# One encoder layer on one core: the order of projection blocks, operand stacks and value transposes in the attention stage

## The chip, the core and the metric

The kernel runs on one core of a Trainium2 chip. The metric is the device time of one execution in microseconds. Three runs of the kernel before give a median of 1028.46 us (1026.88 to 1028.7). The engines are named as in the profile: PE is TensorE (matrix multiply), PEld its weight loads, DVE VectorE, ACT ScalarE, POOL GpSimd, SP the engine that issues most DMAs. L389 is line 389 of the kernel.

## What is computed

One layer of an encoder over 1024 tokens of width 1024, in float32: one projection feeds two kinds of attention, group A (8 heads in two sets of four, a window of 128 tokens to each side) and group B (8 heads, a neighbourhood in a 16 by 64 grid). An output projection and a gated feed-forward block with a convolution follow.

```python
hn = rmsnorm(h, norm_mix[l])
proj = jnp.einsum('bsd,de->bse', hn, w_in[l])
qa, ka, va, qb, kb, vb = jnp.split(proj, splits, axis=-1)
...
o_a = window_gqa_sink(qa, ka, va, sink[l])
o_b = neighbourhood_attention(qb, kb, vb, rpb[l])
mix = jnp.concatenate([rmsnorm(o_a, norm_a[l]), rmsnorm(o_b, norm_b[l])], axis=-1)
h = h + jnp.einsum('bse,ed->bsd', mix, w_out[l])
hn = rmsnorm(h, norm_ffn[l])
h = h + conv_gated_mlp(hn, w_gate[l], w_up[l], conv_w[l], conv_b[l], w_down[l])
return rmsnorm(h, norm_final)
```

## The kernel before

**Arithmetic.** Each float32 operand is split into a rounded high part and the rest. A product is then three matmuls (high by high, rest by high, high by rest: lines 178 to 180). Everything is kept transposed, features on the partitions and tokens along the free dimension.

**Two streams on TensorE.** TensorE's instructions keep the program's order (`manual_schedule`, line 136). The other engines' order is made when the kernel is built, by readiness and priority, so an instruction of theirs can run well ahead of its place in the text. During attention the program interleaves two streams:

- *Filler.* A generator, `rest()` (line 775), runs the jobs. Jobs 3 to 17 are projections (`Project`), each of one 128-column tile; the eight behind them, `OutA`, are the first half of the output projection. A job has 16 *blocks* of three 512-column matmuls (line 177), eight for each half of the tokens. A half is collected in one of two PSUM banks called "pj" and copied out by VectorE (`evacuate`, line 239). Job 17 does both halves side by side; on its way it also splits group A's result for `OutA` (`split_part`, line 608, with line 611 on VectorE).
- *Attention units.* There are 16 window units for group A (two sets of eight) and 32 grid units for group B (four for each of eight heads, units 16 to 47). A unit is a list of events: a score step (two matmuls, line 389, then the softmax: bias and minimum at line 412, exponent at 416, normalisation on GpSimd at 420), a transpose step (lines 452 or 526, then the split at 426 and 427) and a value step (lines 457 and 458, or 537 and 538). Scores run ahead of the transposes by a few steps. The value step that is issued is always that of the transpose before (`pend`).

**Rates.** `RATES` (line 34) sets how many blocks are filled in during each set of window units (first two entries) and each grid head (the other eight). Every event adds its share to `debt`, and whole blocks are issued from it (lines 929 to 932).

**Posts.** When a job's blocks are done, it waits in `waiting` until `settle(age)` (line 758) posts it; the age is the number of the block within the next job. A post needs places for operands (`big(..., "op")`, 14 buffers of 128 by 1024). `needs(m)` says how many; `live["op"]` counts those in use and is lowered by 4 at the end of a grid head (line 933). The rule for the age is in line 765: 3 (`LAG`), 13 for job 3, 1 (`SOON`) for job 17.

- Jobs 6, 9, 12 and 15 are the values of two grid heads each. Their post is `split_v` (line 322): four transposes into a "pj" bank, two copies (line 333) and two subtractions (line 334), and the same again for the second half of the tokens eight settles later (line 347).
- Jobs 7, 8, 10, 11, 13, 14, 16 and 17 are query and key of the grid heads 0 to 7. Their post is `split_qk` (line 296). ScalarE makes the high part in two halves (line 301), VectorE the rest (line 302). Four DMAs on SP's queue then stack high and rest, query and key, into q, ka and kb. Two of them overwrite what the first two read:

```python
nc.sync.dma_start(f32(q[0:64, :]), f32(a[0:64, :]))
nc.sync.dma_start(f32(q[64:128, :]), f32(b[0:64, :]))
mark["stacked"] = nc.sync.dma_start(f32(b[0:64, :]), f32(a[64:128, :]))
nc.sync.dma_start(f32(a[0:64, :]), f32(b[64:128, :]))
```

A head's first score needs all four. `run_q` (line 876) makes sure only that the post has been issued ahead of it in the program. The bias tiles of a grid head are built on GpSimd (lines 490 and 491), on the same queue as the normalisation of line 420.

Of the kernel before, what the change touches and what calls it, by code (L numbers as in the profile page):

```python
# [30 lines left out]

LAG, LATE, SOON = 3, 13, 1
FILL0, FILL1 = 22, 14
RATES = [41, 50, 21, 21, 22, 22, 13, 19, 19, 16]
SPARE = (3, 6)
AHEAD = 4
GRID_AHEAD = 6
# [20 lines left out]
def hybrid_layer(tc, xT, w_first, w_in, w_out, w_gate, w_up, w_down, small, sink, rpb, consts, rope, out):  # L58
    nc = tc.nc
    with ExitStack() as ctx:  # L60
# [11 lines left out]
        slots = {"xg": 16, "op": 14, "mix": 8, "rstd": 1}  # L72
# [28 lines left out]
        flat = lambda t, n: t[:, 0:n * 384].rearrange("p (k c) -> p k c", c=384)  # L101
# [51 lines left out]
        def behind(*names):  # L153

            stack = ExitStack()
            for n in names:
                stack.enter_context(tc.issue_after(mark[n].ins))
            return stack
# [590 lines left out]
        live = {"op": 0}  # L749
        needs = lambda m: 2 if m < 6 and m % 3 else 2 if m >= 6 and m % 3 == 0 else 3  # L750
        waiting = []
# [6 lines left out]
        def settle(age):  # L758

            for item in list(later):  # L760
                item[0] -= 1
                if item[0] <= 0:
                    later.remove(item)
                    item[1]()
            while waiting and (len(waiting) > 1 or age >= (LATE if waiting[0].m == 3 else SOON if waiting[0].m == 17 else LAG)):
                m = waiting[0].m
                if live["op"] + needs(m) > slots["op"]:
                    break
                live["op"] += needs(m)
                with behind(*["stack", "low"] * (m == 3)):  # L770
                    waiting.pop(0).post()
# [3 lines left out]
        def rest():  # L775
            for i, job in enumerate(jobs):
                if i + 1 < len(jobs):
                    with behind(*[["spread", "root"], ["stack"]][i] if i < 2 else []):
                        jobs[i + 1].load()
                for n, _ in enumerate(job.run()):  # L780
                    yield True
                    if i == 0:
                        if n == 8:
                            with behind("copied"):
                                for p in first[:2]:
                                    make_stacks(p)
                        continue
                    if n == REST and i + 1 < len(jobs):
                        jobs[i + 1].load_rest()
                    settle(n)  # L790
                    if (i, n) in aux:
                        aux[i, n]()
                if i == 0:
                    with behind("stack", "copied"):
                        jobs[1].load_rest()
                    with behind("weights", "weights low"):
                        make_stacks(third)
                if isinstance(job, Project):
                    waiting.append(job)
                while len(waiting) > 2:  # L800
                    settle(0)
                    if len(waiting) > 2:
                        yield False
# [34 lines left out]
        def fill(n):  # L838
            while n > 0 and next(filler, False):
                n -= 1  # L840
# [11 lines left out]
        fill(FILL0)  # L852
        rates = RATES
        flat = []
# [13 lines left out]
        def q_until(u, limit):  # L868
            nonlocal qpos
            res = []  # L870
            while qpos < len(queue_q) and queue_q[qpos][0] <= u and len(res) < limit:
                res.append(queue_q[qpos])
                qpos += 1
            return res

        def run_q(items):
            nonlocal debt
            for u, s in items:
                while any(m not in done for m in flat[u][2]):
                    assert next(filler)  # L880
                    debt -= 1
                s()

        sums = {}

        def square_b(u):

            if u == 40:
                sums["b"] = big("sqb", "op")
                for h in range(2):  # L890
                    nc.scalar.activation(sums["b"][:, tsl(h)], mix[4][:, tsl(h)], AF.Square)
            s2 = tmp("sq")
            for h in range(2):
                nc.scalar.activation(s2[:, tsl(h)], mix[5 if u == 40 else 6][:, tsl(h)], AF.Square)
                nc.vector.tensor_tensor(sums["b"][:, tsl(h)], sums["b"][:, tsl(h)], s2[:, tsl(h)], op=ALU.add)

        pend = None
        for i, item in enumerate(q_until(1, 4 + AHEAD)):
            run_q([item])
            fill(i % 2 + 1)  # L900
        fill(FILL1 - 12)
        for u in range(len(flat)):
            q, t, need, kind = flat[u]
            events = []
            if kind == 0:
                mine = q_until(u + 2, 4 if u < 14 else 99)
                for ts in t:
                    events += [("t", ts), ("v", None)]
                for i, item in enumerate(mine):
                    events.insert(min(EVA[i], len(events)), ("q", item))  # L910
                rate = [RATES[u // 8] / 8 / len(events)] * len(events)
            else:
                rate = []
                for ts in t:
                    mine = q_until(len(flat) - 1, 1 if events or u > 16 else GRID_AHEAD - 3)
                    events += [("t", ts)] + [("q", item) for item in mine] + [("v", None)]
                    rate += [RATES[2 + (u - 16) // 4] / 8 / (2 + len(mine))] * (2 + len(mine))
            if u in (40, 44):
                square_b(u)
            for (what, e), per in zip(events, rate, strict=True):  # L920
                if what == "t":
                    nxt = e()
                elif what == "v":
                    if pend is not None:
                        pend()
                    pend = nxt
                else:
                    run_q([e])
                debt += per
                due = max(0, int(debt))  # L930
                fill(due)
                debt -= due
            live["op"] -= 7 if u in (7, 15) else 4 if u >= 16 and u % 4 == 3 else 0
        with tc.high_priority(offset=500), behind("high"):
            nc.scalar.activation(warm, eps, AF.Sqrt)
        fill(2)
# [420 lines left out]
        for i, f in enumerate(FO[HEAD:]):  # L1357
            u = Gated(f)
# [269 lines left out]
```

## Time and profile before

| what | us |
|---|---|
| median of three runs | 1028.46 (1026.88 to 1028.7) |
| profiled execution, its time | 1031.37 |
| profiled execution, its span | 1029.6 |
| DVE busy | 834.8 |
| ACT busy | 563.8 |
| first score of grid head 0 | 170.58 |
| first score of grid head 6 | 300.15 |
| first score of grid head 7 | 325.10 |
| last score | 343.23 |

The span runs from the first to the last instruction. All times in the rows are counted from its start. A row of the timeline gives start, duration, engine, line, operation, output and inputs, and in brackets the idle time before it and what ended that. A row of the windows gives the stretch, its length, the busy time of PE, PEld, DVE, ACT and POOL with the number of instructions, the granted clock of TensorE, the DMA share and GB/s. Matmuls overlap, so what one costs is read from start to start. A wait for several semaphores is put down to the one that came last by the profile.

### The profile page before, as it was taken

How to read it: one execution, taken by the hardware profiler on the slowest of the kernel's cores; microseconds unless marked ns; L12 is line 12 of the kernel's file. 1: busy time of each engine (PE TensorE's matmuls, PEld its weight loads, DVE VectorE, ACT ScalarE, POOL GpSimd, SP SyncE). 2: the span in 40 equal slices, each digit the busy share in tenths (PEclk: the TensorE clock that was granted, in tenths of full speed). 3: DMA queues.
4: the chain of work that ended last, by engine and by line, in shares of the span. 5: the costliest groups of instructions: out<-in, count | busy, mean ns of one | idle time of the engine just before them, and what ended most of it. 6: DMA issues, size and time to landing. Idle time of an engine off the chain costs nothing.

```text
span 1029.6 us, 14879 instructions
## 1 busy us (share of the span) xinstructions
PE 1012.8 (98%) x5094; PEld 893.1 (87%) x5094; DVE 834.8 (81%) x1570; ACT 563.8 (55%) x1081; POOL 107.5 (10%) x188
## 2 busy tenths in 40 slices
PE   9999999999989999999999999999999999999997
PEld 8898888899878988888888888888888888888886
DVE  7889887768978699999987877786787777996675
ACT  8567776657666555555535444443444654554451
POOL 0233342322332100000000000000000000000002
PEclk9999999999989999999999999999999999999998
DMA  7224022333325258313443332333322788966644
GB/s 291 76 77 97 28 72 62 82 82 82 83 61 158 82 166 270 103 41 123 151 187 102 113 117 99 113 113 113 102 98 107 263 303 287 309 243 231 217 161 164
DMA packets 68220, 144.94 MB, mean 141 GB/s; under 512 B 8240, under 2 KB 18736, under 8 KB 68144
## 3 DMA queue, kind: packets, MB, share of 16 engines
q1 hardware_dynamic: 58064, 118.82, 36.1%
q10 hardware_dynamic: 10080, 25.17, 6.3%
q8 instruction: 40, 0.66, 0.3%
q14 instruction: 36, 0.29, 0.1%
HBM read 103.58 MB, written 28.57 MB: 128 GB/s over the span
## 4 chain that ended last, share of the span: by engine, by line
PE 82%; DVE 11%; ACT 3%; DMA 3%; issue 2%; DVEq 0%; POOL 0%; SPq 0%; ACTq 0%
PE pj L178 7%; PE dn L1011 6%; PE dn L1012 6%; PE dn L1013 6%; PE pj L180 6%; PE pj L179 6%; PE x L1011 6%; PE x L1012 6%; PE x L1013 6%; PE y L1011 3%; PE y L1013 3%; PE y L1012 3%; PE s L389 3%; PE z L1013 2%; PE z L1011 2%
## 5 line engine op out<-in xcount | busy, mean ns | idle before, releaser
L1011 PE MATMUL x<-hg,whi 128*128 128x512 f32 x352 | 133.7, 380 | 1.8 <-ACT gs L1053 1.8
L1012 PE MATMUL x<-hg,whi 128*128 128x512 f32 x352 | 133.4, 379 | 0.0
L1013 PE MATMUL x<-hg,wlo 128*128 128x512 f32 x352 | 133.4, 379 | 0.0
L1011 PE MATMUL dn<-xd,whi 128*128 128x512 f32 (+1 forms) x330 | 120.8, 366 | 0.0
L1012 PE MATMUL dn<-xd,whi 128*128 128x512 f32 (+1 forms) x330 | 120.5, 365 | 0.0
L1013 PE MATMUL dn<-xd,wlo 128*128 128x512 f32 (+1 forms) x330 | 120.5, 365 | 0.0
L416 ACT ACTIVATE p<-p,nm 128x385 f32<-128x385 f32 (+3 forms) x128 | 75.1, 587 | 58.0 <-DVE nm L412 55.5
L178 PE MATMUL pj<-xgh,whi 128*128 128x512 f32 x245 | 100.5, 410 | 1.0 <-DVE v L334 0.7
L985 ACT ACTIVATE whi<-ws 128x512 fp32r<-128x512 f32 (+1 forms) x100 | 60.7, 621 | 72.0 <-DVE ws L1125 16.6
L420 POOL TENSOR_SCALAR p<-p,sm 128x384 f32<-128x384 f32 (+1 forms) x128 | 78.3, 625 | 198.3 <-DVE sm L418 158.9
L179 PE MATMUL pj<-xgl,whi 128*128 128x512 f32 x245 | 93.6, 382 | 0.0
L180 PE MATMUL pj<-xgh,wlo 128*128 128x512 f32 x245 | 93.6, 382 | 0.0
L985 ACT ACTIVATE whi<-raw 128x512 fp32r<-128x512 f32 (+1 forms) x102 | 60.9, 610 | 47.3 <-PE x L1012 20.7
L427 DVE TENSOR_TENSOR pl<-pt,ph 128x384 fp32r<-128x384 f32 (+2 forms) x108 | 63.6, 589 | 25.6 <-ACT ph L426 24.0
L986 DVE TENSOR_TENSOR wlo<-ws,whi 128x512 fp32r<-128x512 f32 (+1 forms) x100 | 66.6, 680 | 19.7 <-ACT whi L985 19.5
L1011 PEld LDWEIGHTS x<-hg,whi 128*128 128x128 f32 x352 | 66.5, 189 | 11.9 <-ACT gs L1053 2.6
L1334 DVE TENSOR_TENSOR xd<-xd 128x512 fp32r<-128x512 f32 x77 | 52.3, 687 | 29.2 <-ACT xd L1333 28.8
L1333 ACT ACTIVATE xd<-xd 128x512 fp32r<-128x512 f32 x77 | 47.6, 627 | 51.8 <-DMA xd<-x 50.9
L1448 POOL TENSOR_TENSOR h<-h,wide 128x256 f32<-128x256 f32 (+1 forms) x6 | 5.4, 917 | 673.8 <-ACT wide L1444 673.8
L1013 PEld LDWEIGHTS x<-hg,wlo 128*128 128x128 f32 x352 | 66.5, 189 | 9.5
L1012 PEld LDWEIGHTS x<-hg,whi 128*128 128x128 f32 x352 | 66.5, 189 | 9.4
L986 DVE TENSOR_TENSOR wlo<-raw,whi 128x512 fp32r<-128x512 f32 (+1 forms) x102 | 66.2, 668 | 3.7 <-ACT whi L985 3.7
(267 smaller groups left out, 2532.9 us busy)
## 6 DMA issues: line engine op xcount, KB each, us to landing
xd<-x SPq DMA_DIRECT2D x77, 256.0 KB, 5.0
raw<-in_w_down_dram SPq DMA_DIRECT2D x72, 256.0 KB, 4.5
raw<-in_w_gate_dram SPq DMA_DIRECT2D x22, 512.0 KB, 3.4
raw<-in_w_up_dram SPq DMA_DIRECT2D x22, 512.0 KB, 3.5
x<-c ACTq DMA_DIRECT2D x22, 512.0 KB, 2.6
raw<-in_w_in_dram SPq DMA_DIRECT2D x30, 256.0 KB, 2.7
raw<-in_w_down_dram SPq DMA_DIRECT2D x36, 192.0 KB, 4.2
x<-t ACTq DMA_DIRECT2D x11, 512.0 KB, 2.6
```

The source lines that it names most:

```text
L178: nc.tensor.matmul(ps, w[0], mv(x[0][:, tsl(h)]), start=first, stop=False)
L179: nc.tensor.matmul(ps, w[0], mv(x[1][:, tsl(h)]), start=False, stop=False)
L180: nc.tensor.matmul(ps, w[1], mv(x[0][:, tsl(h)]), start=False, stop=last)
L416: nc.scalar.activation(p[:, j, 0:e], p[:, j, 0:e], AF.Exp, bias=nm, scale=-1.0, accum_out=sm[:, j:j + 1])
L420: nc.gpsimd.tensor_scalar(p[:, i, 0:m], p[:, i, 0:m], sm[:, i:i + 1], 1.0, op0=ALU.mult, op1=ALU.mult)
L427: mark["rest"] = nc.vector.tensor_tensor(pl[:, 0:n], ps[:, 0:n], f32(ph[:, 0:n]), op=ALU.subtract)
L985: nc.scalar.activation(hi, src, AF.Copy)
L986: nc.vector.tensor_tensor(lo, src, f32(hi[:, :, :]), op=ALU.subtract)
L1011: nc.tensor.matmul(ps, w[0], x[0], start=first and i == 0, stop=False, skip_group_check=True)
L1012: nc.tensor.matmul(ps, w[0], x[1], start=False, stop=False, skip_group_check=True)
L1013: nc.tensor.matmul(ps, w[1], x[0], start=False, stop=last and i == len(ws) - 1, skip_group_check=True)
L1334: nc.vector.tensor_tensor(lo, f32(lo), f32(hi), op=ALU.subtract)
```

## The change

Four edits, all in the order in which the attention stage is issued; the instructions stay the same.

```diff
-RATES = [41, 50, 21, 21, 22, 22, 13, 19, 19, 16]
+RATES = [41, 50, 22, 22, 23, 22, 13, 19, 17, 15]
...
-            while waiting and (len(waiting) > 1 or age >= (LATE if waiting[0].m == 3 else SOON if waiting[0].m == 17 else LAG)):
+            while waiting and (len(waiting) > 1 or age >= (LATE if waiting[0].m == 3 else SOON if waiting[0].m >= 16 else LAG)):
                 m = waiting[0].m
-                if live["op"] + needs(m) > slots["op"]:
+                if live["op"] + needs(m) > slots["op"] or m in (6, 9, 12, 15) and age % 8 not in (3, 4):
                     break
...
                 s()
+                if u >= 16 and u % 4 == 3 and s is flat[u][0][-1]:
+                    live["op"] -= 3
...
-            live["op"] -= 7 if u in (7, 15) else 4 if u >= 16 and u % 4 == 3 else 0
+            live["op"] -= 7 if u in (7, 15) else 1 if u >= 16 and u % 4 == 3 else 0
```

1. The rates of grid heads 0, 1 and 2 rise by one block each; those of heads 6 and 7 fall by two and one.
2. Job 16 (query and key of head 6) may be posted at age 1, as job 17 was before, instead of 3.
3. The values of the grid heads (jobs 6, 9, 12, 15) are posted only at ages 3, 4, 11 and 12: near the top of a half.
4. Of the four places that a grid head gives back, three (q, ka, kb) are counted free as soon as its last score has been issued, and one (its values) at the head's end as before.

## The prediction

> **What bounds the kernel now.** I read the page first, then the waits of TensorE, then its timeline around each of those waits, then the chain of waits behind them.
>
> ```profile
> PE 1012.8 (98%) x5094; PEld 893.1 (87%) x5094; DVE 834.8 (81%) x1570; ACT 563.8 (55%) x1081; POOL 107.5 (10%) x188
> ```
>
> ```profile
> PE s L389 <- DMA ka<-kb: 2.5, 1, 2.5
> ...
> PE s L389 <- DMA kb<-ka: 1.5, 2, 0.8
> PE s L389 <- DVE nm L412: 1.1, 2, 0.9
> ...
> PE pj L178 <- DVE v L334: 0.7, 1, 0.7
> ```
>
> TensorE is the bound: it is busy for 1012.8 of 1029.6 us. This change removes and adds no instruction, so all it can win is TensorE's idle time, and clock lost through it. Most of that sits in front of scores (line 389), where a head's stacked operands (q, ka, kb) come late by DMA. The timeline shows where:
>
> ```profile
> 296.47 0.49 PE L526 MATMUL pt<-cst,p 128*128 128x128 f32 x3
> 296.72 0.46 PE L178 MATMUL pj<-xgh,whi 128*128 128x512 f32 x1
> 297.02 0.38 PE L179 MATMUL pj<-xgl,whi 128*128 128x512 f32 x1
> 297.24 0.38 PE L180 MATMUL pj<-xgh,wlo 128*128 128x512 f32 x1
> 300.15 0.35 PE L389 MATMUL s<-ka,q 128*128 128x256 f32 x1 [2.54 <-DMA ka<-kb]
> 301.30 0.58 PE L389 MATMUL s<-kb,q 128*128 128x256 f32 x1 [0.80 <-DMA kb<-ka]
> ```
>
> This is head 6's first score. A 512-column matmul starts 0.22 us after the one before it (297.02 to 297.24) and a 256-column one is taken as half of that, so the second score matmul was due at 297.24 + 0.22 + 0.11 = 297.57. It started at 301.30: **3.73 us late**. Then the clock falls (the last columns are granted clock, DMA share and GB/s):
>
> ```profile
> 300.00:304.00 4.00, 3.05 (x8) 2.55 (x9) 2.93 (x5) 1.23 (x4) 2.83 (x4) 0.59 0.18 38
> 304.00:308.00 4.00, 4.00 (x14) 3.42 (x13) 1.84 (x5) 1.50 (x4) 0.00 (x0) 0.56 0.00 0
> ```
>
> At 0.59 and 0.56 the two stretches lose 0.41 x 4 + 0.44 x 4 = 3.4 us of clock. About 0.4 of it falls in time in which TensorE idled anyway, so **3.0 us** is lost on top of the wait.
>
> ```profile
> 323.85 0.38 PE L180 MATMUL pj<-mgh,wlo 128*128 128x512 f32 x1
> 325.10 0.35 PE L389 MATMUL s<-ka,q 128*128 128x256 f32 x1 [0.87 <-DVE nm L412]
> 326.12 0.38 PE L389 MATMUL s<-kb,q 128*128 128x256 f32 x1 [0.67 <-DMA kb<-ka]
> ```
>
> Head 7's first score: due 323.85 + 0.33 = 324.18, started 326.12, so **1.94 us**. No drop of the clock follows.
>
> ```profile
> 192.27 0.60 PE L329 MATMUL vt<-cst,t 128*128 128x128 f32 x4
> ...
> 195.48 0.45 PE L178 MATMUL pj<-xgh,whi 128*128 128x512 f32 x1 [0.66 <-DVE v L334]
> ```
>
> Job 9's second group of value transposes takes a "pj" bank two blocks before job 11's second half needs one; TensorE waits **0.66 us** for VectorE to empty it. The four places add up to 3.73 + 3.0 + 1.94 + 0.66 = **9.3 us**.
>
> **The change part by part.** TensorE's order is the program's. I worked out by the loop's own arithmetic (rates, debt, ages, count of places) which block of a job stands before which score, with both sets of numbers. For the kernel before, that list agrees with the order of TensorE's rows from job 3's start to the last score.
>
> *The rates* move three blocks of filler from the time of heads 6 and 7 into heads 0 to 2. In all, 281 blocks still stand ahead of the end of the units. Head 6's first score moves from 7 blocks behind job 16's end to 10, and 2 scores, 2 groups of transposes and 2 value pairs also come between. Head 7's moves from 10 blocks behind job 17's end to 12, with 1 score, 1 group and 2 pairs. Prices from job 16's last block:
>
> ```profile
> 288.72 0.33 PE L537 MATMUL o<-ph,v 128*128 128x384 f32 x1
> ...
> 289.04 0.38 PE L178 MATMUL pj<-xgh,whi 128*128 128x512 f32 x1
> ...
> 289.69 0.38 PE L526 MATMUL pt<-cst,p 128*128 128x128 f32 x2
> 289.83 0.41 PE L389 MATMUL s<-ka,q 128*128 128x384 f32 x1
> ...
> 290.24 0.38 PE L178 MATMUL pj<-xgh,whi 128*128 128x512 f32 x1
> ...
> 314.11 0.46 PE L178 MATMUL pj<-mgh,whi 128*128 128x512 f32 x1
> ```
>
> From start to start a value pair takes 0.32 us, a block 0.65, a score 0.41 or less, three transposes 0.25 (296.47 to 296.72). Head 6 so gains 3 x 0.65 + 2 x (0.32 + 0.25 + 0.41) = 3.9 us of lead, head 7 2 x 0.65 + 2 x 0.32 + 0.25 + 0.41 = 2.6. What the stacks need is read from the chain of waits:
>
> ```profile
> 294.57 0.94 DVE kb L302
> ...
> 295.52 2.87 DMA q<-kb
> ...
> 298.40 2.85 DMA kb<-ka
> ...
> 318.33 0.74 DVE kb L302
> ...
> 319.10 2.93 DMA q<-kb
> ...
> 322.04 4.03 DMA kb<-ka
> ```
>
> Two DMAs in series follow the second subtraction. Head 6: job 16's blocks end at 289.69, the stacks land at 298.40 + 2.85 = 301.25, so 11.6 us are needed. There were 297.46 - 289.69 = 7.8, and there will be 11.7: the wait is gone with 0.1 us to spare. Head 7: from 314.11 to 326.07, 12.0 us needed; there were 324.07 - 314.11 = 10.0, and there will be 12.6.
>
> *Posting job 16 at age 1* moves two activations, two subtractions and four DMAs on SP's queue up by two blocks: with the rates, five. But the activation already ran before the old place (block 3 of job 17, TensorE at 294.65):
>
> ```profile
> 292.06 0.72 ACT L301 ACTIVATE ka<-t,cst 128x512 fp32r<-128x512 f32 x1
> ```
>
> Only the end of job 16 holds it, so this edit wins between 0 and the 1 us that the two halves were apart; I take 0. On SP nothing else is issued between the stack's DMAs of head 6, so no transfer is overtaken there. Head 7's stacks keep their place, with a load of w_out's weights between their DMAs.
>
> *Places freed at the last score*: the count only. Without it job 15's post (block 212) would count 12 + 3 = 15 of 14 places and slip; with it, it stays. No other post changes by it: 0.
>
> *Value transposes at a half's top*: of jobs 6, 9, 12 and 15 only job 9 moves, its groups from blocks 126 and 134 to 132 and 140. Each then stands four or more blocks (2.6 us and the attention between) ahead of the next use of a "pj" bank: the 0.66 us go. Four copies and four subtractions move with them, beside job 10's split. That split feeds head 2's first score 23 blocks later, which covers it; were the cover gone, the cost is the 0.7 us back.
>
> **What is late next.** Without the stalls, the same work must fit in less time. VectorE (third busy column):
>
> ```profile
> 230.00:284.00 54.00, 53.86 (x319) 48.41 (x318) 45.25 (x110) 38.89 (x92) 17.39 (x25) 1.00 0.31 80
> 284.00:332.00 48.00, 42.91 (x231) 37.54 (x230) 38.57 (x91) 32.34 (x78) 14.54 (x20) 0.93 0.40 113
> ...
> 430.00:500.00 70.00, 69.11 (x321) 60.20 (x320) 69.64 (x108) 41.00 (x66) 0.00 (x0) 1.00 0.23 74
> ```
>
> Its 38.57 us in 284 to 332 would stand in 48 - 8.7 = 39.3 us: 98%. The trace shows no such load in this stage, so I bound it. If it runs as in 430 to 500 (99%, TensorE idle 0.89 of 70), it costs 0.5 us. If it could be no denser than in 230 to 284 (84%), the stretch would take 46 us and give back 6.6. Some of that work (the split of the first group's mix, line 611) isn't urgent and can slide into the slack behind 332, so I take 1.3, nearer the dense row. GpSimd is the other candidate:
>
> ```profile
> 298.31 1.96 POOL L490 TENSOR_TENSOR xb<-cst,rr 128x384 f32<-128x384 f32 x1 [3.35 <-DVE nm L412]
> ...
> 301.37 1.47 POOL L420 TENSOR_SCALAR p<-p,sm 128x384 f32<-128x384 f32 x2
> ```
>
> The normalisation of head 5's last pair queues behind a bias build. Its first half is through by about 302.4, for a transpose that without the stall is due some 6 us of such pieces behind 297.46, near 303.4: 1 us to spare. I take 0.5 for this and the thin margin of head 6 (from 0 to 2). Sum: 9.3 - 1.3 - 0.5 = 7.5 us. The profiled execution took 1031.37 us (span 1029.6), so it would be 1023.9; the median of the runs shown is 2.9 lower, and 7.5 off 1028.46 is **1021.0**.
>
> **The clock, by trace and rule.** The drop followed idle stretches of 2.54 and 0.80 us, and none followed 0.87 and 0.67. The Trainium skill ("TensorE: Matmul & The Clock Gate", the sections on the clock gate and its oscillation) says that the gate looks at free-running windows of some 3.4 us and that gaps shorter than that keep the clock. The trace disagrees with the second half: no single gap here was that long. By the first half, whether a stall of this size costs clock depends on where the window falls, and may differ from run to run.
>
> **The rivals.**
> *The timed runs have no drop of the clock.* Then 3.0 us can't be won: 7.5 - 3.0 = 4.5, 1024.0. For: the profiled execution is 2.9 us above the median, the size of the drop. Against: nothing else tells the runs apart. 20%.
>
> *VectorE is the bound where the stalls were.* It gives back 6.6 instead of 1.3: 1026.3. For: 98%. Against: the row of 430 to 500. 12%.
>
> *Nothing is won*: the waits move to another head or place in full, 1028.5 (1026.4 to 1030.5). For: ScalarE's and VectorE's orders are made anew at each build, and no row shows the new ones. Against: job ends and DMAs in series set these waits, and both keep their durations. 12%.
>
> *Slower: the splits of line 611 get ahead of head 6's second subtraction in VectorE's queue.*
>
> ```profile
> 296.75 0.67 DVE L611 TENSOR_TENSOR mgl<-mixa,mgh 128x512 fp32r<-128x512 f32 x1
> ```
>
> All eight of them, and job 17's two weight subtractions of like length, would delay it by 10 x 0.67 = 6.7 us. The wait becomes 11.6 + 6.7 - 11.7 = 6.6 against 3.73, the drop of the clock stays, and with 1.8 given back elsewhere and 2.6 won at head 7 and the values, it is 2.9 + 1.8 - 2.6 = 2.1 us slower: 1030.6. It turns slower from nine such instructions on. Against: line 611 writes places that job 17 frees two blocks at a time, and it ran behind the subtraction before. 9%.
>
> **How the numbers follow.** The forecast, 1021.0, has 47%; its own range, with 0.5 to 3.6 given back, is 1019.6 to 1022.8. With the case without the drop and most of the VectorE case, 1018.5 to 1027.0 holds 8 in 10. A measurement of this kernel tells some 0.2% (2.06 us) from no change: faster means below 1026.4. That holds the forecast, the first rival and most of the second: 0.78; same 0.12; slower 0.10.
>
> **What would show it.** TensorE's waits list the DMAs of ka and kb with under 0.5 us in all; the granted clock is 1.00 from 296 to 308; the row of "pj" waiting for the value subtraction is gone; the span from head 6's job to the end of the units is some 9 us shorter, and the rest of the trace is shifted by that. It is wrong if line 389 still waits over 2 us, if line 526 or 537 begins to wait, or if the gain vanishes later, between 430 and 500.

## The result and the profile after

The changed kernel takes 1021.99 us (median of six runs, 1021.22 to 1024.5) against 1029.33 for the kernel before (six runs): a ratio of 0.9926, with a 95% interval of 0.9912 to 0.9939. That is 7.3 us less; 7.5 were forecast.

The profiled execution spans 1022.7 us. It lost 1.75 us where nothing was changed, ahead of the first value step, and is the slowest of its six runs. Most of that is the clock's: by the trace's clock records it first rose to full 10.0 us behind the start, against 7.1 in the kernel before, and in the 2.9 us between TensorE ran nine matmuls instead of 15. So the attention stage is read by itself. These are its first and last value steps in TensorE's timeline, first of the kernel before:

```profile
70.00 0.38 PE L457 MATMUL o<-ph,v 128*128 128x512 f32 x1
...
357.45 0.28 PE L538 MATMUL o<-pl,v 128*128 128x256 f32 x1
```

and then of the changed kernel:

```profile
71.75 0.38 PE L457 MATMUL o<-ph,v 128*128 128x512 f32 x1
...
350.64 0.28 PE L538 MATMUL o<-pl,v 128*128 128x256 f32 x1
```

287.45 us have become 278.89: the stage is 8.56 us shorter. Where they came from is in TensorE's waits of the changed kernel (line numbers behind 882 are two higher):

```profile
PE x L1013 <- ACT gs L1055: 1.6, 2, 0.9
...
PE s L389 <- DMA kb<-ka: 1.0, 2, 0.6
...
PE s L389 <- DVE nm L412: 0.2, 1, 0.2
```

Of the four rows shown in the prediction, the wait for ka (2.5 us) and the one of "pj" for the value subtraction (0.7) are gone, the one for kb has gone from 1.5 to 1.0, and that for line 412 from 1.1 to 0.2. The timeline around head 6's and head 7's first scores:

```profile
297.18 0.38 PE L180 MATMUL pj<-xgh,wlo 128*128 128x512 f32 x1
...
299.47 0.27 PE L389 MATMUL s<-ka,q 128*128 128x256 f32 x1
300.35 0.38 PE L389 MATMUL s<-kb,q 128*128 128x256 f32 x1 [0.61 <-DMA kb<-ka]
...
319.35 0.36 PE L389 MATMUL s<-ka,q 128*128 128x256 f32 x1
320.06 0.38 PE L389 MATMUL s<-kb,q 128*128 128x256 f32 x1 [0.36 <-DMA kb<-ka]
```

Head 6's second score matmul starts 0.88 us behind the first, where 0.11 would do: 0.8 us late instead of 3.7. Head 7's starts 0.71 us behind its first, where behind a group of transposes 0.19 would do: it is 0.5 us late instead of 1.9. The clock stays up behind both, and VectorE stays busier (windows of the changed kernel; third busy column, then the clock two columns further):

```profile
300.00:304.00 4.00, 3.65 (x20) 3.37 (x21) 4.00 (x11) 1.81 (x6) 2.82 (x4) 1.00 0.27 112
304.00:308.00 4.00, 4.00 (x26) 3.63 (x26) 3.86 (x11) 3.42 (x10) 2.39 (x4) 1.00 0.15 45
...
284.00:332.00 48.00, 46.94 (x273) 41.82 (x272) 42.33 (x103) 35.90 (x90) 16.55 (x25) 1.00 0.47 132
```

So 3.73 - 0.8 = 2.9 and 1.94 - 0.5 = 1.4 us come from the two waits, 0.7 from the values and 3.0 from the clock (0.59 and 0.56 before: 3.4 us, of which some 0.4 fell in the wait and is counted there). That is 8.0 of the 8.56 us. The rest is smaller waits; one of them, 0.2 us of line 178 for line 246 ahead of head 6, is gone from the rows too.

What head 6 still waits for shows in the chain of waits of the changed kernel:

```profile
293.78 0.68 DVE kb L302
...
294.48 2.83 DMA q<-kb
...
297.32 2.98 DMA kb<-ka
...
300.35 0.38 PE s L389
```

The two DMAs take what they took before (2.83 + 2.98 against 2.87 + 2.85). The subtraction ahead of them is what is late: it begins 5.8 us behind the job's end instead of 4.8 (the table behind the experiments).

### The profile page after: what moved, and what is told of

The parts are those of the page before. It is cut to its first block, busy times and chain, and to the rows that moved or that the text cites. A ratio compares the mean times of both kernels' runs of the same rounds, so it can differ in the third digit from the quotient of the medians.

```text
span 1022.7 us, 14878 instructions
## 1 busy us (share of the span) xinstructions
PE 1010.2 (99%) x5094; PEld 891.6 (87%) x5094; DVE 834.5 (82%) x1570; ACT 561.7 (55%) x1081; POOL 107.3 (10%) x188
## 4 chain that ended last, share of the span: by engine, by line
PE 83%; DVE 10%; ACT 3%; issue 2%; DMA 2%; DVEq 0%; POOL 0%; SPq 0%; ACTq 0%; POOLq 0%
PE pj L178 7%; PE pj L180 7%; PE pj L179 7%; PE dn L1015 7%; PE dn L1013 7%; PE dn L1014 7%; PE x L1013 6%; PE x L1014 6%; PE x L1015 6%; PE y L1015 3%; PE y L1014 3%; PE y L1013 3%; PE s L389 3%; PE z L1015 2%; PE z L1013 2%
## 5 line engine op out<-in xcount | busy, mean ns | idle before, releaser
L1013 PEld LDWEIGHTS x<-hg,whi 128*128 128x128 f32 x352 | 66.5, 189 | 11.8 <-ACT gs L1055 2.4
L1014 PEld LDWEIGHTS dn<-xd,whi 128*128 128x128 f32 x330 | 62.5, 189 | 7.7
```

What stands on the lines that cost most here:

```text
L1013: nc.tensor.matmul(ps, w[0], x[0], start=first and i == 0, stop=False, skip_group_check=True)
L1014: nc.tensor.matmul(ps, w[0], x[1], start=False, stop=False, skip_group_check=True)
```

## The experiments

Each ratio is that of a kernel to the kernel before on the same chip, with its 95% interval.

**1. The rates alone.**

```diff
-RATES = [41, 50, 21, 21, 22, 22, 13, 19, 19, 16]
+RATES = [41, 50, 22, 22, 23, 22, 13, 19, 17, 15]
```

> The kernel before with the new rates alone. Theory (a head's first score waits for its job's end plus some 11.6 us of subtractions and two DMAs in series; only the blocks in between count): head 6's wait falls from 3.3 us of idle time to under 0.7 and head 7's from 1.5 to under 0.5, granted clock 1.00 behind head 6, job 9's wait of 0.66 stays. The count of places now lets job 15's values go only at block 215, its second group at 223, one block before job 17 needs a pj bank, so a new wait of 0.7 to 1.3 us there. Sum some -6.5 us, ratio 0.992 to 0.995. Rival (the place of the post counts, two of the five blocks come from the age): head 6 still waits for over 1.2 us, ratio 0.995 to 0.998.

Measured: 1023.72 us, ratio 0.9944 (0.9931 to 0.9958). No wait for ka or kb is left among TensorE's waits:

```profile
PE pj L178 <- DVE t L246: 1.7, 1, 1.7
...
PE pj L178 <- DVE v L334: 0.4, 1, 0.4
```

The first row is new. In TensorE's timeline it stands behind job 15's *first* value group, which now takes a bank one block ahead of the second half of job 16 (the expectation had put it at the second group, and lower):

```profile
275.02 0.60 PE L329 MATMUL vt<-cst,t 128*128 128x128 f32 x4
278.25 0.48 PE L178 MATMUL pj<-xgh,whi 128*128 128x512 f32 x1 [1.65 <-DVE t L246]
```

The rates are the part that brings the gain, and they bring a cost of their own with them: by its timeline job 15's first group stands three blocks later than in the kernel before.

**2. Job 16 posted at age 1, alone.**

```diff
-SOON if waiting[0].m == 17 else LAG
+SOON if waiting[0].m >= 16 else LAG
```

> The kernel before with job 16 posted at age 1, nothing else. Theory: nothing, head 6's wait stays within 0.5 us of 3.3 us, ratio 0.998 to 1.002. Rival (the place of the post counts): two blocks with what stands between are 2.6 us, so the wait falls below 1.5 us, no drop of the clock, -3 to -5.5 us, ratio 0.995 to 0.997.

Measured: 1029.93 us, ratio 1.0003 (0.9993 to 1.0013). The wait for ka is there again with 2.5 us. The age is worth nothing by itself.

**3. The rule for the values alone.**

```diff
-                if live["op"] + needs(m) > slots["op"]:
+                if live["op"] + needs(m) > slots["op"] or m in (6, 9, 12, 15) and age % 8 not in (3, 4):
```

> The kernel before with the rule for the age of value posts alone: only job 9 moves. Theory: the wait of pj for the value subtraction (0.66 us) goes, nothing else moves: -0.7 us, ratio 0.998 to 1.000, head 6's wait as before. Rival (value copies crowd the stacks, and their move is what helps heads 6 and 7): waits at heads 6 and 7 fall by over 1 us.

Measured: 1029.81 us, ratio 0.9999 (0.999 to 1.0008). The row of "pj" waiting for line 334 is gone, and heads 6 and 7 wait as before; 0.7 us can't be told in the time.

**4. The changed kernel with the old rates.**

```diff
-RATES = [41, 50, 22, 22, 23, 22, 13, 19, 17, 15]
+RATES = [41, 50, 21, 21, 22, 22, 13, 19, 19, 16]
```

> The changed kernel with the old rates: ages, places and value rule stay. Theory: the gain is gone but for the 0.7 us at job 9: head 6 waits 3.3 us again, with half the clock behind it; ratio 0.997 to 1.001. Rival (the place of the post or of the values counts): at least 3 us of the 7.3 us gain stay, ratio below 0.997.

Measured: 1029.82 us, ratio 0.9999 (0.999 to 1.0008). Without the rates the other three edits bring nothing that can be measured.

Three of these also show, beside the kernel before, how the clock behaves. Head 6 idles for about the same 3.3 us (2.5 and 0.8) in the kernel before and in experiments 2, 3 and 4, but what follows differs. The same window of the kernel before, of experiment 2 and of experiment 3 (granted clock in the third column from the right):

```profile
300.00:308.00 8.00, 7.05 (x21) 5.96 (x22) 4.78 (x9) 2.73 (x7) 2.83 (x4) 0.57 0.09 19
```

```profile
300.00:308.00 8.00, 7.33 (x43) 6.70 (x44) 6.16 (x14) 3.67 (x9) 3.26 (x5) 1.00 0.01 3
```

```profile
300.00:308.00 8.00, 7.65 (x33) 6.73 (x34) 4.64 (x11) 3.83 (x9) 2.76 (x5) 0.79 0.00 0
```

They lose 0.43 x 8 = 3.4 us, nothing, and 0.21 x 8 = 1.7 us; experiment 4 loses 3.4 like the kernel before. Head 7's wait costs clock too in experiment 3 (0.79 in 324 to 332) and in experiment 2 (0.92 in 316 to 324, 0.86 in the next 8 us), 1.7 us each; in the kernel before and in experiment 4 it doesn't.

The traces' clock records tell the cases apart. In the attention stage every drop begins a whole number of stretches of 3.41 us, called *windows* here, behind the clock's first rise (86, 87, 93 or 94 of them), and lasts one window or two. TensorE's idle time in those windows, for head 6's stall (experiments 9 and 11 are told below):

| kernel | idle in the window of the stall, us | in the next window, us | half clock from the next window on, us |
|---|---|---|---|
| before | 2.73 | 0.61 | 6.83 |
| old rates (4) | 2.53 | 0.73 | 6.83 |
| values (3) | 2.63 | 0 | 3.41 |
| one block back (9) | 2.88 | 0 | 3.41 |
| before, splits first (11) | 2.48 | 0 | 3.41 |
| age (2) | 1.88 | 1.45 | 0 |

Where one window holds most of the stall, the next one runs at half clock, and where 0.6 or 0.7 us of the stall reach into that one, so does a second. In experiment 2 the border cuts the stall in two, and nothing follows. Head 7's stall fits: a drop behind 1.86 and 1.98 us of idle time in one window (experiments 2 and 3), none behind 1.19 to 1.58 (before, experiments 4, 9 and 11). So the limit in this stage lies near 1.9 us of 3.41, an estimate (1.88 us in experiment 2 had no drop behind it). At the kernel's end, among other matmuls, the clock also falls behind windows with less, 1.10 us in experiment 8, so idle time is not the whole rule. This is read from the profiles; no run moved the border on purpose.

**5. The rates with the places freed at the last score.** Experiment 1, and with it:

```diff
                 s()
+                if u >= 16 and u % 4 == 3 and s is flat[u][0][-1]:
+                    live["op"] -= 3
...
-            live["op"] -= 7 if u in (7, 15) else 4 if u >= 16 and u % 4 == 3 else 0
+            live["op"] -= 7 if u in (7, 15) else 1 if u >= 16 and u % 4 == 3 else 0
```

> The kernel before with the new rates and the places freed at the last score: job 15's values go at block 212 again, job 9's stay at 126. Theory (the count of places is worth what the slipped values of job 15 cost under the rates alone): the wait of 1.7 us for a pj bank is gone, the 0.4 to 0.7 us at job 9 stay, heads 6 and 7 wait for under 1 us together; some 1.5 us below the rates alone, ratio 0.992 to 0.994. Rival (the prediction's price of 0 for this edit): the wait of 1.7 us stays and the ratio is that of the rates alone, 0.9944.

Measured: 1022.7 us, ratio 0.9927 (0.9915 to 0.9939). The new wait of 1.7 us is gone, job 9's stays:

```profile
PE s L389 <- DMA kb<-ka: 1.3, 2, 0.7
...
PE pj L178 <- DVE v L334: 0.4, 1, 0.4
```

Heads 6 and 7 wait a little more than expected (1.3 us, not under 1). The places are the edit that takes the rates' own cost away: the row shows it, while the intervals of the two times overlap. The opposite, the changed kernel without the freed places, was not tried; by the loop's arithmetic job 15's second group would then fall into job 17, which holds both "pj" banks, and TensorE would wait for a bank that only its own later blocks give up.

**6. The changed kernel with job 16 posted at age 3.** Line 765 as before, all else as changed.

> The changed kernel with job 16 posted at age 3 as before. Theory (the place of the post is worth nothing): head 6 waits no more than in the changed kernel (0.6 us) give or take 0.5, no drop of the clock, ratio 0.9915 to 0.9935. Rival (the five blocks count together): head 6 waits over 1.5 us, ratio 0.994 or more.

Measured: 1022.03 us, ratio 0.992 (0.9907 to 0.9933). Head 6 waits 0.6 us, as in the changed kernel. The age does nothing in this company either: of the "five blocks" that the prediction names for the post, the three of the rates count.

**7. One block instead of three**, on the kernel before:

```diff
-RATES = [41, 50, 21, 21, 22, 22, 13, 19, 19, 16]
+RATES = [41, 50, 21, 21, 23, 22, 13, 19, 18, 16]
```

> The kernel before with one block of filler moved instead of three (head 2's rate up by one, head 6's down by one). Theory (the wait falls by what is put between the job and the score): one block, and a value pair or a transpose group with it, are 1.0 to 1.6 us, so head 6 is late by 2.1 to 2.7 us instead of 3.7 and head 7 by 0.3 to 0.9 instead of 1.9; job 15's values go at block 213. With less idle time the clock drops seldom: ratio 0.996 to 0.998. Rival (the stacks follow the post, which stays 3 blocks ahead plus one): the same at head 6, nothing at head 7. Second rival (VectorE sets the wait): head 6's wait stays above 3.2 us.

Measured: 1025.12 us, ratio 0.9951 (0.9937 to 0.9964), a little better than the expected 0.996 to 0.998. TensorE's timeline:

```profile
297.34 0.38 PE L180 MATMUL pj<-xgh,wlo 128*128 128x512 f32 x1
298.11 0.35 PE L389 MATMUL s<-ka,q 128*128 128x256 f32 x1 [0.39 <-DVE pl L427]
299.75 0.38 PE L389 MATMUL s<-kb,q 128*128 128x256 f32 x1 [1.30 <-DMA kb<-ka]
```

The second score matmul was due at 297.34 + 0.33 = 297.67 and is 2.1 us late, the lower end of what was expected; head 7 is 0.75 late. The clock is 1.00 behind it.

**8. Three more blocks**, on the changed kernel:

```diff
-RATES = [41, 50, 22, 22, 23, 22, 13, 19, 17, 15]
+RATES = [41, 50, 23, 23, 24, 22, 13, 19, 16, 13]
```

> The changed kernel with three more blocks moved the same way (rates 23, 23, 24, ..., 16, 13). Theory: only the 1.0 us that heads 6 and 7 still wait can be won, so 0 to 1 us below the changed kernel, ratio 0.991 to 0.9927. Rival (the last heads get too few blocks to cover the softmax and VectorE is full there): new waits at lines 526 or 537 of over 1 us, ratio above 0.9935.

Measured: 1022.14 us, ratio 0.9921 (0.9908 to 0.9934). Heads 6 and 7 don't wait for ka or kb any more, but other rows have come in their place:

```profile
PE pj L178 <- DVE v L334: 0.7, 1, 0.7
...
PE o L538 <- DVE pl L427: 0.4, 1, 0.4
```

The row for line 334 is not job 9's: it stands at 275.75, behind job 15's first group. Nothing is won over the changed kernel that can be measured.

**9. One block back**, on the kernel before:

```diff
-RATES = [41, 50, 21, 21, 22, 22, 13, 19, 19, 16]
+RATES = [41, 50, 21, 21, 21, 22, 13, 19, 20, 16]
```

> The kernel before with one block moved the other way (head 2's rate down by one, head 6's up by one): head 6's first score comes 6 blocks behind its job instead of 7, head 7's 9 instead of 10. Theory: both are later by the 1.0 to 1.6 us that one block and what stands with it are worth: head 6 by 4.7 to 5.3 us, head 7 by 2.9 to 3.5, with half the clock behind head 6 in all profiles and behind head 7 in some; +1.5 to +5 us, ratio 1.0015 to 1.005. Rival (the wait at head 6 is not set by the job's end): no change, 0.999 to 1.001.

Measured: 1028.97 us, ratio 0.9992 (0.9979 to 1.0004): a miss, and the number that the rival gave. Head 6 has one block less of lead and is late by 3.65 us, no more than before; head 7, too, is late by 1.97 us, as before. For head 6 the timeline on VectorE says why:

```profile
290.95 0.68 DVE L246 TENSOR_TENSOR t<-pj,rstd 128x512 f32<-128x512 f32 x1
...
292.43 1.66 DVE L302 SCALAR_TENSOR_TENSOR kb<-t,cst,ka 128x512 fp32r<-128x512 f32 x2
294.01 0.68 DVE L611 TENSOR_TENSOR mgl<-mixa,mgh 128x512 fp32r<-128x512 f32 x1
```

The two subtractions (line 302) run back to back here. In the kernel before, the chain shows the second one from 294.57, 3.4 us behind the last evacuation at 291.15; here it begins about 2.1 us behind. In the changed kernel (VectorE's timeline) a step of head 4's result, a split and a softmax step stand between the two:

```profile
288.98 0.69 DVE L246 TENSOR_TENSOR t<-pj,rstd 128x512 f32<-128x512 f32 x1
...
290.82 0.75 DVE L302 SCALAR_TENSOR_TENSOR kb<-t,cst,ka 128x512 fp32r<-128x512 f32 x1
...
292.05 0.79 DVE L554 TENSOR_TENSOR mixb<-o,ot 64x512 f32<-64x512 f32 x1 [0.40 <-ACT ot L552]
292.75 0.56 DVE L427 TENSOR_TENSOR pl<-pt,ph 128x384 fp32r<-128x384 f32 x1
293.21 0.56 DVE L412 CUSTOM_DVE_ANT_0 p<-s,xb 128x384 f32<-128x384 f32 x1
...
293.69 0.76 DVE L302 SCALAR_TENSOR_TENSOR kb<-t,cst,ka 128x512 fp32r<-128x512 f32 x1
```

These three are not the whole delay. The subtraction needs ScalarE's second high part, and ScalarE's timeline of the changed kernel has a softmax step, a step of head 4's result and a split between the two as well:

```profile
290.08 0.71 ACT L301 ACTIVATE ka<-t,cst 128x512 fp32r<-128x512 f32 x1
...
292.43 0.71 ACT L301 ACTIVATE ka<-t,cst 128x512 fp32r<-128x512 f32 x1
```

The second one ends at 293.14, so VectorE's own order costs the last 0.5 us. From one high part to the next it is 2.35 us here, 1.48 in the kernel before (292.06 to 293.54) and 0.63 in this experiment (291.67 to 292.30). The order on VectorE and ScalarE is made anew for each kernel, and the time from a job's end to the second subtraction moves with it.

**10. One more block**, on the changed kernel:

```diff
-RATES = [41, 50, 22, 22, 23, 22, 13, 19, 17, 15]
+RATES = [41, 50, 22, 22, 23, 23, 13, 19, 16, 15]
```

> The changed kernel with one more block moved ahead of heads 6 and 7 (head 3's rate 23, head 6's 16). Theory: the 0.6 us that head 6 and the 0.4 us that head 7 still wait are gone, 0 to 1 us below the changed kernel, ratio 0.991 to 0.9925. Rival (TensorE has no more to win there, another wait takes their place as with three more blocks): 0.992 to 0.9935.

Measured: 1022.5 us, ratio 0.9929 (0.9917 to 0.9941). Heads 6 and 7 wait no more, and line 538 waits for the split of line 427 instead:

```profile
PE o L538 <- DVE pl L427: 1.1, 2, 0.8
```

The rival expected this.

**11. The splits put first**, on the kernel before:

```diff
-            for h in range(2):
-                nc.scalar.activation(a[:, tsl(h)], t[:, tsl(h)], AF.Copy, scale=by)
-                nc.vector.scalar_tensor_tensor(b[:, tsl(h)], t[:, tsl(h)], by, f32(a[:, tsl(h)]), op0=ALU.mult, op1=ALU.subtract)
             with tc.high_priority(offset=500):
+                for h in range(2):
+                    nc.scalar.activation(a[:, tsl(h)], t[:, tsl(h)], AF.Copy, scale=by)
+                    nc.vector.scalar_tensor_tensor(b[:, tsl(h)], t[:, tsl(h)], by, f32(a[:, tsl(h)]), op0=ALU.mult, op1=ALU.subtract)
```

> The kernel before with the two halves of the grid heads' operand split (lines 301 and 302) put ahead in ScalarE's and VectorE's order, no block moved. Theory, as it stands after one block back (a head is late by the time from its job's end to the second subtraction, plus the 0.8 to 1.0 us to the DMA and some 6 us for two DMAs in series, less the lead of its blocks): the second subtraction comes 3 to 3.6 us behind job 16's end instead of 4.8, so head 6 is late by 1.9 to 2.6 us instead of 3.7 with the lead unchanged at 7.8; head 7 likewise by about a microsecond less; the clock drops less often; -2 to -4.5 us, ratio 0.9955 to 0.998. Rival (the lead alone counts): late by 3.7 again, 0.999 to 1.001.

Measured: 1026.32 us, ratio 0.9964 (0.995 to 0.9977). No block is moved, and the kernel is 0.36% faster. The chain of waits (the subtraction's line is now 303):

```profile
292.10 1.42 DVE kb L303 x2
...
293.54 3.29 DMA q<-kb
...
296.85 2.84 DMA kb<-ka
...
299.73 0.38 PE s L389
```

The second subtraction begins 3.8 us behind job 16's end instead of 4.8, and head 6 is 2.9 us late instead of 3.7. That is less than expected (1.9 to 2.6 us late): the subtraction came 3.8 us behind the end where 3 to 3.6 were expected, and the first DMA took 3.29 instead of 2.87 us.

**12. The splits put first**, on the changed kernel.

> The changed kernel with the same order for the splits. Theory: the second subtraction comes 3 to 3.6 us behind job 16's end instead of 5.8, heads 6 and 7 don't wait, 0 to 1 us below the changed kernel, ratio 0.991 to 0.9925. Rival (what the splits overtake is late instead): waits for the softmax or the split of the transposes (lines 389, 526, 537, 538) take the place, 0.992 to 0.9945.

Measured: 1022.32 us, ratio 0.9926 (0.9911 to 0.9941). Heads 6 and 7 don't wait; line 538 does, by 1.0 us in two places. As in experiments 8 and 10, the last microsecond changes its place. No version is measurably below the changed kernel.

**What the twelve give together.** From the timelines, for head 6: the lead is the time from the end of job 16's last block to the place of the second score matmul without a wait; the other columns count from the same end.

| kernel | blocks between | lead, us | second subtraction begins | score matmul starts | late |
|---|---|---|---|---|---|
| one block back (9) | 6 | 6.9 | 3.5 | 10.5 | 3.65 |
| before | 7 | 7.9 | 4.8 | 11.6 | 3.7 |
| before, splits first (11) | 7 | 7.9 | 3.8 | 10.7 | 2.9 |
| one block (7) | 8 | 8.9 | 4.4 | 11.0 | 2.1 |
| changed (10 blocks) | 10 | 11.7 | 5.8 | 12.4 | 0.8 |
| changed, age 3 (6) | 10 | 11.7 | 5.8 | 12.4 | 0.75 |
| rates alone (1) | 10 | 12.2 | 3.5 | 12.2 | 0 |
| changed, splits first (12) | 10 | 11.8 | 3.6 | 11.8 | 0 |

In the six kernels of the table that wait, the start of the second subtraction and the score matmul are 6.6 to 7.0 us apart: the subtraction and two DMAs. What a head waits is that, plus the start of the subtraction, less the lead. The lead is set by the blocks. The start of the subtraction swings between 3.5 and 5.8 us with the order on VectorE and ScalarE. Experiments 2, 3 and 4 repeat the row of the kernel before, and experiment 5 that of the changed kernel, within 0.1 us.

## Why the prediction was right, point by point

- **The bound and the price of the four waits.** Right. Of the 9.3 us, 8.0 came out of the stage in the profiled pair; what is left is head 6's 0.8 and head 7's 0.5. The DMAs of ka and kb are still waited for by 1.0 us in all, where the prediction's sign was under 0.5; its other signs came: the clock of 1.00, the row of "pj" gone, and no new wait at line 526 or 537.
- **The rates carry it.** Right: 0.9944 alone, 0.9999 without them. The lead of head 6 grew from 7.8 to 11.6 us (11.7 was worked out).
- **"11.6 us are needed" for head 6's stacks.** This term was taken as fixed and was mis-sized: 12.4 in the changed kernel, because the second subtraction starts 5.8 us behind the job's end and not 4.8. The "0.1 us to spare" became 0.8 us of wait. The size was covered by the 0.5 us taken for thin margins, by its range more than by its reason. Head 7 went the same way: it was given 0.6 us to spare and is 0.5 late, since from job 17's last block to the score it took 13.65 us instead of 12.26. Its second subtraction starts 5.1 us behind that block instead of 4.5, and its last DMA takes 4.8 instead of 4.1 from issue to score. The miss of experiment 9 comes from the same step: it changed the lead by 1.0 us and left the other term alone, which moved by 1.3 the other way.
- **VectorE gives back 1.3 us.** Mis-sized: no such wait shows. In 284 to 332 the changed kernel runs 273 matmuls with VectorE busy for 42.33 of the 48 us; the kernel before needs 54.81 us for 272 matmuls from 284 on, with 43.74 us of VectorE's work. So VectorE runs at 88% instead of 80%, and about 1.4 us of its work moved further back, where it had room. The prediction named this slack and still took 1.3. Where VectorE is full (15.78 of the 16 us of 292 to 308), it is the order of its work that makes the stacks late and not the load: in experiment 1 it is busy for all of 292 to 300, with the second subtraction at 3.5 us.
- **GpSimd is late next.** Not seen: no wait of TensorE ends on line 420.
- **The age is worth 0.** Right, in both companies (experiments 2 and 6).
- **The freed places cost and bring 0.** Right as a count (job 15 keeps block 212), but the price of the slip that they prevent was not worked out. It is the 1.7 us wait of experiment 1, which experiment 5 takes away.
- **The values at a half's top: 0.66 us.** Job 9's wait is gone wherever the rule is in; the time can't tell it. In experiment 11 it shrinks to 0.15 us without the rule.
- **The clock.** The prediction took 3.0 us in full and gave 20% to a case in which the timed runs have no such drop. Neither is quite so: the drop comes and goes. In the 70 runs of the kernel before that stand beside the experiments, the mean granted clock of a run was 0.993 to 0.998, and the span follows it on average: 1029.9 us at 0.993 (seven runs), 1028.4 at 0.995 (22), 1027.1 at 0.996 (17) and 1026.0 at 0.998 (three), though runs of one clock differ by some 3 us. The six runs of the changed kernel are all at 0.997 or 0.998. By these averages a run of the kernel before loses between nothing and some 4 us to the clock, about 2.4 in the middle, and that would be the part of the median's 7.3 us that isn't idle time.
- **The total.** That 7.3 us came so near to 7.5 is luck in part. The 1.8 us given back to VectorE, GpSimd and the thin margins nearly balanced what came in their place: the 1.3 us still waited for the stacks, and some 0.6 us of clock that a middling run of the kernel before doesn't lose (2.4 in place of 3.0).
- **The slower rival.** Line 611 did not get ahead of the second subtraction: in the changed kernel it follows at 294.35. But the mechanism behind that rival, other work getting between the two halves of the split, is real: the second subtraction's start moves by up to 2.3 us (3.5 to 5.8).

## What to carry to other kernels

Where one engine's order is written by hand and the others' is made by a scheduler, a distance in the hand-written order is only half of a wait's price; the other half, the time that the producer takes, moves when the order is made anew, and has to be read again from each new profile. When moved work makes something slip that is counted (places, banks), look for what it slips into: the 1.7 us here came from one group of value transposes that took a bank at the wrong block. A short stall of TensorE costs more than its length where the clock can fall behind it: here up to 3.4 us more, by where the stall lies in the clock's windows.

## What the runs showed of the hardware

The same stall (2.5 and 0.8 us of idle time with one short matmul between) was followed by 3.4 us, 1.7 us or nothing of lost clock in four profiles, in which TensorE's order around it is the same. At half the clock that is 6.83, 3.41 or 0 us of time. This agrees with the Trainium skill ("TensorE: Matmul & The Clock Gate", the sections on the clock gate and its oscillation), by which the gate judges activity over free-running windows of some 3.4 us. Its rule against drops, no idle gap over some 3.4 us, was not enough here: no single gap was over 2.54 us, and 1.86 us of idle time in one window, in two gaps, were followed by a drop. The kernel before ran over 4.3 us of spread (1027.29 to 1031.59 in 29 runs), the changed one over 3.3 (1021.22 to 1024.5 in six), of which 2.35 are between its first, profiled run and the next slowest. Six runs are few, so the spread is not shown to be smaller.
